# First projections from raw fp32 chunks, the gates' arithmetic on GpSimd, and other ranks in the mixer of a two-layer decoder trunk

## The chip, the core and the metric

The kernel runs on one core of a Trainium2 chip. The metric is the time of one execution in device microseconds; the time before is 652.5 us, the median of three runs (650.82, 652.57, 652.5). PE is TensorE, DVE is VectorE, ACT is ScalarE, POOL is GpSimd; SP is the engine whose queue issues most of the loads.

## What is computed

Two layers on x of 256 tokens by 1024, all in float32. Layer 0 mixes tokens with a gated DeltaNet, layer 1 with softmax attention; after each mixer and after each SwiGLU (hidden width 2816) stands a residual with alpha = sqrt(2) and a LayerNorm. The change touches layer 0's mixer:

```python
proj = x @ w_in                       # q, k, v, z: 1024 columns each; b and a: 8 each
qkv = silu(causal_depthwise_conv(qkv, w_conv))      # width 4
q = l2_normalize(q) * 128 ** -0.5;  k = l2_normalize(k)
beta = sigmoid(b_logit)
g = -(exp(a_log) * softplus(a_in + dt_bias))        # the gates
gc = cumsum(g) in chunks; decay[c, s] = exp(gc[c] - gc[s]) for s <= c
low = strict_tril((k * beta) @ k.T * decay)         # triangular solve per chunk
sol = triangular_solve(low, [v * beta, k * beta * exp(gc)])
o = (chunked recurrence with sol, q, k, decay)
o = o * rsqrt(mean(o * o) + 1e-6) * norm_g * silu(z)
x = LN(alpha * x + o @ w_out)
```

## The kernel before

**Weights.** All weights lie in DRAM as 204 units of 128 x 1024 floats in the order of use, two units to a chunk of 1 MB. A chunk is loaded into one of three `raw` buffers (`Stream.load`; the first two chunks in pieces by `Stream.first`). Each unit is then split for full precision: ACT rounds it to `hi` (`Stream.head`), DVE makes `lo = raw - hi` (`Stream.rest`), into one of nine buffer pairs; the first `NSMALL` units are split in two halves. x is split alike, into `xTh` and `xTl`. A product of 128 x 128 weights with 256 tokens is three fp32r matmuls: hi by xTh, hi by xTl, lo by xTh; a unit of eight is 24 (`proj_w`).

**Layer 0's mixer.** `ORDER` is the order of the projections: `k0` is two units (256 columns of k), `z0` four units in two passes. After each part a job runs beside the stream: `keys`, `queries`, `values` do the convolution (`conv_silu`: two ACT copies with scale, six DVE scalar_tensor_tensor from PSUM, then a Silu that waits for the mark `decay`), transposes (`ptk`, `ptq`, `ptv`) and small products. `gram` is a product of kT with itself, times `dT` it gives `gdT`; `blocks` inverts its 16 x 16 diagonal blocks on DVE with trips through DRAM (`dG`, `dX`, `dXT`; `cB` is its first DVE step); `doubling` grows the inverse with small products (`py`, `pz0`, `pz1`); `core` is the recurrence; then `wo` follows.

**The gates.** `pgate` is x times the 16 gate columns in fp32; a DVE copy, two products (`pgate2`) and a copy give `ba`; `gates` then works out g on tiles of 128 x 16: exponentials on ACT, the rest on DVE, a series for the softplus, down to `gg`. Four products (`pcum`) sum it up. Their first row goes to DRAM (`d1`, the DMA `d<-gT`), comes back spread over all partitions (`grow`, four loads, one in each job `decay`), is masked by four POOL selects into `dT` and passes through 16 ACT exponentials. When all are done, `grow` itself is exponentiated and `decay` is marked.

**Order.** There is no scheduler on the chip that could reorder: each engine runs its instructions in the order in which the program writes them, and waits on semaphores. That order is worked out when the program is written: `Clock` keeps a modelled time for each engine from the costs in `act`, `tt`, `ptt`, `select`, `mm`, and `dma`; after each matmul of the main stream `tick` looks which jobs' next steps would be ready and takes, on each engine, the one with the lowest rank. Ranks are `PR` (by kind of job), `GET_PRIO` (for splits, by how far ahead of their use they are) and `LOAD_PRIO` (chunk loads on SP). PSUM is two groups of four banks, `A` and `P`.

**The start.** Eight warm-up products; on SP's queue `wg` (the gate weights) and the first pieces of the chunks; on ACT's queue four loads of x and two of `al` (a_log and dt_bias), then the activation table's load. The first two units and x are split in halves as they come, with five warm-up products after each of the first two pairs of gate products.

Of the kernel before, what the change touches and what calls it, by code (L numbers as in the profile page):

```python
# [12 lines left out]
F32 = mybir.dt.float32  # L13
# [5 lines left out]
P = 128  # L19
# [4 lines left out]
H = 8  # L24
# [12 lines left out]
NWARM = (8, 5, 5, 0, 0)  # L37
NSMALL = 40
# [87 lines left out]
def trunk_kernel(ctx: ExitStack, tc: tile.TileContext, xT, xtok, wst, wgate, conv, alog, dtb,  # L126
# [28 lines left out]
    def act(out_, in_, func=AF.Copy, after=0.0, **kw):  # L155
        base = 0.09 + 0.00083 * width(out_)
        base += 0.06 * any(not isinstance(kw.get(a, 1.0), float) for a in ("scale", "bias"))
        base += 0.095 * ("accum_out" in kw)
# [35 lines left out]

    def pmemset(out_, v):
# [34 lines left out]
    class Stream:  # L230
        def __init__(self):
            self.raw, self.hi, self.lo = {}, {}, {}
            self.loaded = self.piece = self.freed = 0
            self.late, self.first_at = [], {}
# [7 lines left out]
            self.pieces[1:3] = self.pieces[2:0:-1]  # L242
# [44 lines left out]
        def head(self):  # L287
            u, a, b = self.pieces[self.piece]
            if a == 0:
                self.hi[u] = wp.tile([P, UCOLS], F32R, tag="hi", name=f"hi{u}", bufs=NHL)  # L290
                self.lo[u] = wp.tile([P, UCOLS], F32R, tag="lo", name=f"lo{u}", bufs=NHL)
# [78 lines left out]
    def tick():  # L370
        polled = set()
        while True:
# [4 lines left out]
            for eng in ("pe", "act", "dve", "pool", "sp"):  # L377
# [10 lines left out]
                elif eng == "sp" and ws.pend:  # L388
# [240 lines left out]
    warm(NWARM[0])  # L629
# [3 lines left out]
    xt = []  # L633
# [6 lines left out]
    al = cst.tile([P, 2, H], F32, name="al")  # L640
    nc.scalar.dma_start(al[:, 0], bass.AP(tensor=alog.tensor, offset=alog.offset, ap=[[0, P], [1, H]]))
    nc.scalar.dma_start(al[:, 1], bass.AP(tensor=dtb.tensor, offset=dtb.offset, ap=[[0, P], [1, H]]))
    ws.first(4, 11.5)
    ws.first(5, 13.0)
# [7 lines left out]

    ea = cst.tile([P, H], F32, name="ea")
    act(ea[:, 0:1], ones[:, 0:1], AF.Exp)
    T.update(act=4.5, pe=0.0)
# [16 lines left out]
    T["pool"] = 3.0  # L672
# [20 lines left out]
    def gates(pg):  # L693
# [14 lines left out]
        tt(xa, ba[:, 1], al[:, 1, :, None].to_broadcast([P, H, 2]), OP.add)  # L708
# [4 lines left out]
        act(ea, al[:, 0], AF.Exp)  # L713
        yield

        ts(s2, at, 2.0, None, OP.add)
        ts(gt[:, 0], gt[:, 0], 1.0, None, OP.add)
        recip(s2, s2)
        recip(beta, gt[:, 0])
        tt(at, at, s2, OP.mult)  # L720
        ts(xa, xa, 0.0, None, OP.max)
        tt(s2, at, at, OP.mult)
        tt(xa, xa, ea[:, :, None].to_broadcast([P, H, 2]), OP.mult)
        ts(acc, s2, 1.0 / 15, None, OP.mult)
        tt(at, at, ea[:, :, None].to_broadcast([P, H, 2]), OP.mult)
# [19 lines left out]
        dma(nc.sync, d1, gT)  # L745
        bT = cst.tile([16, P], F32, name="bT")
# [10 lines left out]
        yield from wait(*[("decay", j) for j in range(4)])  # L757
        g1 = grow.rearrange("p (h c) t -> p h c t", c=2)[:, :, 1]
        act(g1, g1, AF.Exp)
        mark("decay")  # L760
# [13 lines left out]
        select(cmask[:, P:], cmask[:, P:], [[-1, P]], OP.is_ge, NEG, 1)  # L774

    def decay(j, d1, ngc):
# [4 lines left out]
            bass.AP(tensor=d1.tensor, offset=d1.offset + 512 * j, ap=[[0, P], [1, 512]]), 0.73)  # L781
# [34 lines left out]

    kT = b8("kT", [P, H, SEQ])
# [240 lines left out]
    def values(j, ps, pname):  # L1058
        vt = yield from t2(f"vt{j}", (P, 2, SEQ))
        yield from conv_silu(vt, ps, pname, 16 + 2 * j, f"v{j}")  # L1060
        yield from wait("nk", "q")
# [14 lines left out]
    def core(G):  # L1076
# [4 lines left out]
        zz = big_t["zz"]  # L1081
# [8 lines left out]
        def fin(c, pname, ps):  # L1090
# [9 lines left out]
            yield from wait(("z", G, c))  # L1100
            for i in range(4):
# [42 lines left out]
    def gates_z(G, t, pz):  # L1144
# [364 lines left out]
```

## Time and profile before

| | us |
|---|---|
| median of three timed runs | 652.5 |
| the profiled execution | 651.09 |
| its span, from the first to the last instruction | 649.3 |
| PE busy in the span | 636.8 |
| DVE, ACT, POOL busy | 458.4, 366.7, 29.9 |

The span is what the profile's rows cover; the rest of the profiled execution's time lies around it. A matmul's end in the rows is modelled, so groups that overlap in the rows can be read by the distance of their starts.

### The profile page before, as it was taken

What the parts mean: (1) busy time and instruction counts of PE and PEld (TensorE: products, weight loads), DVE (VectorE), ACT (ScalarE), POOL (GpSimd) and SP (SyncE); (2) the same over time, 40 slices, a digit from 0 to 9 for tenths busy, and PEclk for the clock granted to TensorE, in tenths of its full rate; (3) what the DMA queues carried; (4) which work ended last, traced back from release to release, by engine and by line L of the source; (5) the groups of instructions that cost most, each with busy time, mean ns of one, the idle gap of its engine ahead of it and who ended that gap; (6) DMA issues with size and microseconds to landing.
All of it is one profiled execution on the core that took longest, in us unless ns stands there. A gap on an engine that the chain in (4) does not pass through costs nothing.

```text
span 649.3 us, 9918 instructions
## 1 busy us (share of the span) xinstructions
PE 636.8 (98%) x3791; PEld 555.1 (85%) x3791; DVE 458.4 (71%) x802; ACT 366.7 (56%) x719; POOL 29.9 (5%) x43
## 2 busy tenths in 40 slices
PE   8999999999999999999999999999999999999995
PEld 7999898898888888888888888888888888888884
DVE  3878999368976666666649679887886666666645
ACT  4689757874465555555535468765475555555510
POOL 1043100021000000000000000000000000000001
PEclk9999999899999999999999999999999999999998
DMA  8576478145655555555545474352565555555302
GB/s 285 194 257 165 138 211 249 50 155 179 251 219 216 175 188 186 192 195 187 198 191 194 143 268 174 132 194 70 191 258 200 191 194 195 195 194 189 136 0 66
DMA packets 37024, 117.91 MB, mean 182 GB/s; under 512 B 20464, under 2 KB 21648, under 8 KB 23536
## 3 DMA queue, kind: packets, MB, share of 16 engines
q1 hardware_dynamic: 35376, 115.54, 50.6%
q10 hardware_dynamic: 1440, 1.58, 0.8%
q8 instruction: 30, 0.49, 0.3%
q0 software_dynamic: 160, 0.15, 0.2%
q14 instruction: 18, 0.15, 0.1%
HBM read 115.41 MB, written 1.85 MB: 181 GB/s over the span
## 4 chain that ended last, share of the span: by engine, by line
PE 91%; issue 6%; ACT 1%; DVE 1%; POOL 0%; DVEq 0%; POOLq 0%; ACTq 0%
PE pf L213 31%; PE acc L213 17%; PE pqk L213 7%; PE pz L213 4%; PE pu L213 4%; PE pcvalues L213 4%; PE bo L213 3%; PE wo L213 3%; PE pg L213 3%; PE pv L213 3%; PE pcqueries L213 2%; PE pl L213 2%; PE po L213 2%; PE sc L213 1%; PE lnT L216 1%
## 5 line engine op out<-in xcount | busy, mean ns | idle before, releaser
L172 DVE TENSOR_TENSOR lo<-raw,hi 128x1024 fp32r<-128x1024 f32 (+1 forms) x244 | 252.8, 1047 | 116.4 <-ACT hi L166 114.7
L166 ACT ACTIVATE hi<-raw 128x1024 fp32r<-128x1024 f32 (+1 forms) x244 | 219.7, 924 | 165.4 <-issue 59.2
L213 PE MATMUL pf<-xT,hi 128*128 128x512 f32 x576 | 143.8, 391 | 0.0
L213 PEld LDWEIGHTS pf<-xT,hi 128*128 128x128 f32 x576 | 104.6, 189 | 19.4
L213 PE MATMUL acc<-hi,ht 128*128 128x512 f32 x320 | 99.0, 391 | 0.0
L213 PEld LDWEIGHTS pf<-xT,lo 128*128 128x128 f32 x576 | 78.6, 190 | 5.6
L213 PE MATMUL pf<-xT,lo 128*128 128x256 f32 x576 | 80.8, 283 | 0.0
L213 PEld LDWEIGHTS acc<-hi,ht 128*128 128x128 f32 x320 | 59.0, 188 | 11.4
L213 PE MATMUL acc<-lo,ht 128*128 128x512 f32 x160 | 62.3, 390 | 0.0
L213 PEld LDWEIGHTS acc<-lo,ht 128*128 128x128 f32 x160 | 30.0, 188 | 6.3
L213 PE MATMUL pqk<-xT,hi 128*128 128x512 f32 x128 | 34.7, 401 | 0.0
L172 DVE TENSOR_TENSOR sgw<-sgw,pf 128x256 f32<-128x256 f32 x72 | 29.8, 415 | 1.6 <-ACT sgw L166 1.6
L193 POOL TENSOR_TENSOR lnst<-lnst,nhalf 128x1 f32<-128x1 f32 x8 | 8.5, 1057 | 488.4 <-DVE lnst L180 488.4
L166 ACT ACTIVATE sgw<-pf 128x256 f32<-128x256 f32 x72 | 26.4, 366 | 0.0
L213 PEld LDWEIGHTS pqk<-xT,hi 128*128 128x128 f32 x128 | 22.8, 189 | 3.7
L213 PE MATMUL pckeys<-xT,hi 128*128 128x256 f32 x128 | 23.7, 286 | 0.5 <-ACT hi L166 0.5
L213 PE MATMUL pcqueries<-xT,hi 128*128 128x256 f32 x128 | 23.8, 287 | 0.0
L213 PE MATMUL pcvalues<-xT,hi 128*128 128x256 f32 x128 | 23.1, 283 | 0.0
L176 DVE SCALAR_TENSOR_TENSOR y<-y,lnst,gb 128x512 f32<-128x512 f32 (+1 forms) x36 | 22.7, 685 | 0.0
L213 PE MATMUL pz<-hi,xT 128*128 128x512 f32 x64 | 22.1, 417 | 0.0
L213 PEld LDWEIGHTS pckeys<-xT,hi 128*128 128x128 f32 x128 | 19.9, 191 | 1.1 <-ACT hi L166 1.1
L213 PE MATMUL pu<-hi,xT 128*128 128x512 f32 x64 | 20.4, 395 | 0.0
(233 smaller groups left out, 999.5 us busy)
## 6 DMA issues: line engine op xcount, KB each, us to landing
raw<-wst SPq DMA_DIRECT2D x100, 1024.0 KB, 4.8
gb<-lnp SPq DMA_DIRECT2D x4, 1024.0 KB, 7.0
xraw<-xT ACTq DMA_DIRECT2D x4, 256.0 KB, 5.9
raw<-wst SPq DMA_DIRECT2D x4, 256.0 KB, 5.4
raw<-wst SPq DMA_DIRECT2D x2, 512.0 KB, 6.4
grow<-d SPq DMA_DIRECT2D x4, 256.0 KB, 6.3
y<-xtok SPq DMA_DIRECT2D x1, 1024.0 KB, 7.1
out_dram<-y ACTq DMA_DIRECT2D x4, 128.0 KB, 1.9
```

Of the source, the lines that this page charges most:

```text
L166: return op("act", cost, lambda: nc.scalar.activation(out_, in_, func, **kw), after)
L172: return dve(out_, 0.06 + 0.00105 * rate * width(out_), lambda: nc.vector.tensor_tensor(out_, a, b, op=alu), after)
L176: lambda: nc.vector.scalar_tensor_tensor(out_, a, s, b, op0=op0, op1=op1), **kw)
L193: op("pool", cost, lambda: nc.gpsimd.tensor_tensor(out_, a, b, op=alu))
L213: op("pe", cost, lambda: nc.tensor.matmul(out_, lhs, rhs, start=start, stop=stop, **kw))
L216: op("pe", 0.11, lambda: nc.tensor.transpose(out_, src, ident[:src.shape[0], :src.shape[0]]))
```

## The change

The first halves of units 0 and 1 are multiplied in fp32 straight from the loaded chunk and from raw x (`first_step`); the second halves and x are split in a new order, and the warm-up products after the first eight are gone. All eight gate products stand together, before the last step of units 0 and 1. `al` is loaded on POOL's queue, `wg` after the first chunk, and the table load stands between the second and third load of x. The gates' elementwise work goes to POOL except the two reciprocals. No chunk load may be written on SP between the write of `d1` and the last load of `grow` (`held`). `gates` waits for the four `decay` jobs only after its own DMAs. Costs in the model, ranks and `ORDER` are new (`v0` after `q0`, `v1` and `z0` after `q3`), and 56 units are split in halves in place of 40.

```diff
-NWARM = (8, 5, 5, 0, 0)
-NSMALL = 40
+NWARM = 8
+NSMALL = 56
-GET_PRIO = (3.5, 3.3), (4.5, 0), (12.5, 5.9), (17.0, 3.6), (18.0, 11.7)
-LOAD_PRIO = 6.35
+GET_PRIO = (-3.5, 3), (2.5, 4.3), (17.5, 8.6), (19.0, 3.6), (33.5, 8.9)
+LOAD_PRIO = 9.85
-PR = dict(gates=2.5, decay=5.2, blocks=0, doubling=1, core=2.5, out0=3.2, z=1, k=2.6, q=4.0, v=1.4, late=3.0, ln=0, ffn=5.6, att=4.4)
+PR = dict(gates=0, decay=6.4, blocks=0, doubling=6.0, core=0, out0=0, z=2.8, k=1.1, q=5.7, v=2.3, late=5.0, ln=0, ffn=5.6, att=4.4)
-ORDER = "k0 k1 k2 k3 q0 q1 q2 q3 z0 v0 v1 v2 v3 z1"
+ORDER = "k0 k1 k2 k3 q0 v0 q1 q2 q3 v1 z0 v2 v3 z1"
...
+    def pts(out_, a, s0, s1, op0, op1=None):
+        kw = {} if op1 is None else dict(op1=op1)
+        op("pool", 0.15 + 0.0025 * width(out_), lambda: nc.gpsimd.tensor_scalar(out_, a, s0, s1, op0=op0, **kw))
...
-        op("pool", 0.12 + 0.0015 * width(out_),
+        op("pool", 0.12 + 0.00205 * width(out_),
...
-                elif eng == "sp" and ws.pend:
+                elif eng == "sp" and ws.pend and not ws.held:
...
-    nc.sync.dma_start(wg, wgate)
-    for n in range(4):
+    for n, t in enumerate((4.2, 4.7, 6.0, 7.0)):
         k = slice(2 * n, 2 * n + 2)
         nc.scalar.dma_start(xraw[:, k], xT[:, k])
-        xt += [4.7 + 1.45 * n] * 2
-        ws.first((0, 2, 1, 3)[n], 5.4 + 1.5 * n)
-    nc.scalar.dma_start(al[:, 0], bass.AP(tensor=alog.tensor, offset=alog.offset, ap=[[0, P], [1, H]]))
+        ws.first((0, 2, 1, 3)[n], t)
+        if n == 1:
+            act(ea[:, 0:1], ones[:, 0:1], AF.Exp)
+    nc.sync.dma_start(wg, wgate)
+    nc.gpsimd.dma_start(al[:, 0], bass.AP(tensor=alog.tensor, offset=alog.offset, ap=[[0, P], [1, H]]))
...
-        tt(xa, ba[:, 1], al[:, 1, :, None].to_broadcast([P, H, 2]), OP.add)
+        ptt(xa, ba[:, 1], al[:, 1, :, None].to_broadcast([P, H, 2]), OP.add)
...
-        ts(acc, s2, 1.0 / 15, None, OP.mult)
-        for m in (13, 11, 9, 7, 5, 3):
-            stt(acc, acc, 1.0 / m, s2, OP.add, OP.mult)
-        stt(acc, acc, 1.0, at, OP.add, OP.mult)
-        stt(gg, acc, -2.0, xa, OP.mult, OP.subtract)
+        pts(acc, s2, 1.0 / 15, 1.0 / 13, OP.mult, OP.add)
+        for m in (11, 9, 7, 5, 3, 1):
+            ptt(acc, acc, s2, OP.mult)
+            pts(acc, acc, 1.0 / m, None, OP.add)
+        ptt(acc, acc, at, OP.mult)
+        ptt(gg, acc, nea[:, :, None].to_broadcast([P, H, 2]), OP.mult)
...
         dma(nc.sync, d1, gT)
+        then(lambda: setattr(ws, "held", 4))
...
+    def first_step(u, n):
+        raw = ws.raw[0][:, u * UCOLS:(u + 1) * UCOLS].rearrange("p (k c) -> p k c", c=P)
+        for k in (2 * n, 2 * n + 1) if n < 2 else ():
+            mm(first_ps[:, u], raw[:, k], xraw[:, k], start=u == k == 0, stop=False, skip_group_check=True)
+        if n < 2:
+            return
+        hi, lo = (c[u].rearrange("p (k c) -> p k c", c=P) for c in (ws.hi, ws.lo))
+        for i, (a, b) in enumerate(((hi, xTh), (hi, xTl), (lo, xTh))):
+            for k in (2 * n, 2 * n + 1):
+                mm(first_ps[:, u], a[:, k], b[:, k], start=False, stop=k == KT - 1 and i == 2, skip_group_check=True)
...
+    x_part(0)
+    x_part(1)
+    w_part(0)
+    x_part(2)
+    w_part(1)
+    x_part(3)
```

What stands in a row on PE at the program's start, first before, then after (`pckeys` is the bank of units 0 and 1):

```order
L627 MATMUL pwarm<-ones 128x128 x8
L213 MATMUL pgate<-xraw,wg 32x256 x2
L627 MATMUL pwarm<-ones 128x128 x5
L213 MATMUL pgate<-xraw,wg 32x256 x2
L627 MATMUL pwarm<-ones 128x128 x5
L213 MATMUL pckeys_154<-xT_136,hi_164 128x256 x2
L213 MATMUL pckeys_154<-xT_136,lo_165 128x256
```

```order
L635 MATMUL pwarm<-ones 128x128 x8
L221 MATMUL pckeys_154<-xraw,raw_90 128x256 x8
L221 MATMUL pckeys_154<-xT_136,hi_159 128x256 x4
L221 MATMUL pckeys_154<-xT_136,lo_160 128x256 x2
L221 MATMUL pckeys_154<-xT_136,hi_165 128x256 x4
L221 MATMUL pckeys_154<-xT_136,lo_166 128x256 x2
L221 MATMUL pgate<-xraw,wg 32x256 x8
L221 MATMUL pckeys_154<-xT_136,hi_159 128x256 x4
L221 MATMUL pgate_205<-sum_115,l_148 128x16 x2
```

Eight products from `raw` come first, all gate products stand behind them, and `pgate2` follows after four more. `pcum` stood after 15 products of unit 4 and now stands between units 3 and 4.

On DVE behind the second reciprocal of the gates, before and after (`lo` is a split of weights, `cyk` the convolution of k, `gt` the gates' tile, `gT` the copy that waits for `pcum`):

```order
L186 RECIPROCAL beta<-gt 128x16
L172 TENSOR_TENSOR gt<-gt 128x16
L180 TENSOR_SCALAR gt<-gt 128x16
L176 SCALAR_TENSOR_TENSOR cyk_251<-pckeys_154,cw,cyk_251 128x254
L172 TENSOR_TENSOR gt<-gt 128x16
L172 TENSOR_TENSOR gt<-gt,ea 128x16
L176 SCALAR_TENSOR_TENSOR cyk_251<-pckeys_154,cw,cyk_251 128x253
L180 TENSOR_SCALAR gt<-gt 128x16
L172 TENSOR_TENSOR lo_292<-raw_105,hi_291 128x512
```

```order
L186 RECIPROCAL beta<-gt 128x16
L176 SCALAR_TENSOR_TENSOR cyk_237<-pckeys_154,cw,cyk_237 128x255
L172 TENSOR_TENSOR lo_257<-raw_107,hi_256 128x512
L176 SCALAR_TENSOR_TENSOR cyk_237<-pckeys_154,cw,cyk_237 128x255
L172 TENSOR_TENSOR lo_257<-raw_107,hi_256 128x512
L176 SCALAR_TENSOR_TENSOR cyk_237<-pckeys_154,cw,cyk_237 128x254 x2
L172 TENSOR_TENSOR lo_272<-raw_107,hi_271 128x512
L176 SCALAR_TENSOR_TENSOR cyk_237<-pckeys_154,cw,cyk_237 128x253
L172 TENSOR_TENSOR lo_272<-raw_107,hi_271 128x512
L176 SCALAR_TENSOR_TENSOR cyk_237<-pckeys_154,cw,cyk_237 128x253
L172 TENSOR_TENSOR lo_315<-raw_206,hi_314 128x512
L183 COPY gT<-pcum 16x128
```

The gates' small operations are gone from DVE; five splits stand between the reciprocals and `gT`.

On POOL from the masks of `dT` on, before and after (`d` is the write of the beta rows, `bB` their way back, `dX` and `dXT` are cleared in DRAM):

```order
L200 AFFINE_SELECT dT<-grow 128x512 x4
L224 DMA d_384<-bT 16x128
L224 DMA bB<-d_384 64x16 x2
L196 MEMSET l_148 64x256
L224 DMA dX<-l_148 64x16x16
```

```order
L193 TENSOR_TENSOR gg<-gt,nea 128x16
L232 DMA d_346<-bT 16x128
L208 AFFINE_SELECT dT<-grow 128x512 x3
L232 DMA bB<-d_346 64x16 x2
L204 MEMSET l_148 64x256
L232 DMA dX<-l_148 64x16x16
L232 DMA dXT<-l_148 64x16x16
L204 MEMSET misc 128x256
L204 MEMSET misc 128x16
L204 MEMSET cmask 128x256
L208 AFFINE_SELECT cmask<-cmask 128x128
L208 AFFINE_SELECT dT<-grow 128x512
```

Ahead of `gg` stand 23 more operations of the gates; the fourth select has moved behind the gates' DMAs and memsets. On SP, `d1` stood two chunk loads ahead of the four loads of `grow`, and now stands right ahead of them.

## Rows read from the trace of the kernel before

**Rows 1.** The page's first part: busy time of each engine.
```profile
PE 636.8 (98%) x3791; PEld 555.1 (85%) x3791; DVE 458.4 (71%) x802; ACT 366.7 (56%) x719; POOL 29.9 (5%) x43
```
**Rows 2.** Stretches: length, busy PE, PEld, DVE, ACT, POOL; granted clock, DMA share, GB/s.
```profile
113.80:117.00 3.20, 3.20 (x13) 2.69 (x12) 2.29 (x7) 2.99 (x6) 0.00 (x0) 0.50 0.57 236
...
160.00:200.00 40.00, 40.00 (x201) 33.59 (x200) 33.71 (x41) 22.66 (x28) 0.99 (x1) 1.00 0.63 230
```
**Rows 3.** Who PE waited for: us in total, times, longest.
```profile
PE gram L213 <- ACT kT L166: 1.2, 1, 1.2
...
PE py L213 <- issue: 0.7, 1, 0.7
PE pcum L213 <- DVE gg L176: 0.7, 1, 0.7
```
**Rows 4.** The first 24 us in order of time: start, us, engine, instruction, idle before.
```profile
6.87 1.28 ACT L166 ACT_TABLE_LOAD   x1 [6.87 <-DMA xraw<-xT]
...
7.60 1.38 PE L627 MATMUL pwarm<-ones 128*128 128x128 f32 x10
...
8.27 0.61 ACT L166 ACTIVATE xT<-xraw 128x512 fp32r<-128x512 f32 x1
...
9.46 0.59 PE L213 MATMUL pckeys<-xT,hi 128*128 128x256 f32 x2 [0.48 <-ACT hi L166]
...
13.09 0.64 PE L213 MATMUL pgate<-xraw,wg 128*32 128x256 f32 x8
...
23.02 0.84 ACT L166 ACTIVATE cyk<-pckeys,cw 128x256 f32<-128x256 f32 x2 [1.48 <-PE pckeys L213]
```
**Rows 5.** The loads of x, and stretches of the first 8 us (GB/s last).
```profile
L637 ACTq DMA_DIRECT2D xraw<-xT x4: 414/452/453, 0.8 to 2.2; - x4
...
DMA to landing us min/median/max: 4.3/5.9/7.0
...
0.00:4.00 4.00, 2.96 (x14) 2.96 (x15) 0.00 (x0) 0.00 (x0) 1.89 (x14) 1.00 0.46 110
4.00:6.00 2.00, 1.47 (x10) 0.87 (x10) 0.00 (x0) 0.00 (x0) 0.00 (x0) 1.00 0.99 360
6.00:8.00 2.00, 2.00 (x17) 1.47 (x17) 0.00 (x0) 1.13 (x1) 0.00 (x0) 1.00 1.06 399
```
**Rows 6.** The chain that ended last: fp32 products of 128 columns, fp32r ones of 256.
```profile
73.14 0.89 PE pa L213 x8
...
82.77 23.03 PE pcvalues L213 x192
```
**Rows 7.** DVE in order of time: the end of the gates' chain.
```profile
25.11 0.18 DVE L176 SCALAR_TENSOR_TENSOR gg<-gt 128x16 f32<-128x16 f32 x1
```
**Rows 8.** POOL and DVE in order of time; groups of `pow`, ns min/median/max.
```profile
1.49 1.01 POOL L663 TENSOR_SCALAR_AFFINE_SELECT sum<-sum 128x16 f32<-128x16 f32 x4
...
L193 POOL TENSOR_TENSOR lnst<-lnst,nhalf x8: 907/952/1433, 158.3 to 643.2; 128x1 f32<-128x1 f32 x8
...
L193 POOL TENSOR_TENSOR ms<-ms,nhalf x4: 1008/1014/1391, 134.5 to 146.3; 128x4 f32<-128x4 f32 x4
...
37.53 1.30 POOL L200 TENSOR_SCALAR_AFFINE_SELECT dT<-grow 128x512 f32<-128x512 f32 x1 [34.69 <-DMA grow<-d]
37.66 0.67 DVE L172 TENSOR_TENSOR lo<-raw,hi 128x512 fp32r<-128x512 f32 x1
...
39.83 0.63 POOL L200 TENSOR_SCALAR_AFFINE_SELECT dT<-grow 128x512 f32<-128x512 f32 x1
```
**Rows 9.** SP, POOL and ACT in order of time, on the way to the mark `decay`.
```profile
27.90 3.48 SPq L250 DMA_DIRECT2D raw<-wst  x2
...
46.02 1.05 POOL L224 DMA_DIRECT2D bB<-d  x2 [3.87 <-DMA d<-bT]
...
50.20 0.29 POOL L200 TENSOR_SCALAR_AFFINE_SELECT cmask<-cmask 128x128 f32<-128x128 f32 x1
...
47.17 0.63 ACT L166 ACTIVATE kT<-cyk 128x512 f32<-128x512 f32 x1
```

More of the change, by code (lines that the diff above doesn't have):

```diff
@@ L157, in act @@
         base += 0.06 * any(not isinstance(kw.get(a, 1.0), float) for a in ("scale", "bias"))
-        base += 0.095 * ("accum_out" in kw)
+        base += 0.095 * ("accum_out" in kw) + 0.035 * (not isinstance(kw.get("bias", 1.0), float))
         def cost():
@@ L233, in __init__ @@
             self.loaded = self.piece = self.freed = 0
-            self.late, self.first_at = [], {}
+            self.late, self.first_at, self.held = [], {}, 0
             self.arrive, self.ready, self.job = {}, {}, Job()
@@ L288, in head @@
             u, a, b = self.pieces[self.piece]
-            if a == 0:
+            if u not in self.hi:
                 self.hi[u] = wp.tile([P, UCOLS], F32R, tag="hi", name=f"hi{u}", bufs=NHL)
@@ L651, in trunk_kernel @@
     nc.sync.dma_start(rp, rope)
-    ea = cst.tile([P, H], F32, name="ea")
-    act(ea[:, 0:1], ones[:, 0:1], AF.Exp)
-    T.update(act=4.5, pe=0.0)
+    T.update(act=4.1, pe=0.0)
     ident = cst.tile([P, P], F32, name="ident")
@@ L756, in gates @@
         mark("e2")
[L757 to L760, printed above, removed]
         yield
@@ L774, in gates @@
         select(cmask[:, P:], cmask[:, P:], [[-1, P]], OP.is_ge, NEG, 1)
+        yield from wait(*[("decay", j) for j in range(4)])
+        g1 = grow.rearrange("p (h c) t -> p h c t", c=2)[:, :, 1]
+        act(g1, g1, AF.Exp)
+        mark("decay")
+        yield
     def decay(j, d1, ngc):
@@ L780, in decay @@
         dma(nc.sync, grow[:, c].rearrange("p a b -> p (a b)"),
-            bass.AP(tensor=d1.tensor, offset=d1.offset + 512 * j, ap=[[0, P], [1, 512]]), 0.73)
+            bass.AP(tensor=d1.tensor, offset=d1.offset + 512 * j, ap=[[0, P], [1, 512]]), 0.95)
+        then(lambda: setattr(ws, "held", ws.held - 1))
         yield
@@ L1060, in values @@
         yield from conv_silu(vt, ps, pname, 16 + 2 * j, f"v{j}")
-        yield from wait("nk", "q")
+        yield from wait("nk", *["q"] * z_first)
         pt = yield from to_tokens(vt, f"ptv{j}")
@@ L1144, in gates_z @@
     def gates_z(G, t, pz):
+        yield from wait("decay", *["q"] * (not z_first))
         if "zz" not in big_t:
             big_t["zz"] = b8("zz", [P, 2, D])
-        yield from wait("decay")
         act(big_t["zz"][:, t, 512 * G:512 * G + 512], pz, AF.Silu)
@@ L1179, in trunk_kernel @@
     first_ps = main_bank("P", "pckeys0").rearrange("p (a b) -> p a b", a=2)
[L1180 to L1201 removed]
+    def first_step(u, n):
[8 more added lines that the diff above has]
+                mm(first_ps[:, u], a[:, k], b[:, k], start=False, stop=k == KT - 1 and i == 2, skip_group_check=True)
+                if n == 3:
+                    tick()
@@ new lines, in trunk_kernel, with made, x_part, w_part @@
+    at = {}
+    def made(name):
+        at[name] = T["dve"] + LAT - 0.48
+    def x_part(n):
+        c = slice(2 * n, 2 * n + 2)
+        split(xTh[:, c], xTl[:, c], xraw[:, c], xt[2 * n])
+        made(("x", n))
+    def w_part(u):
+        ws.head()
+        ws.rest()
+        made(("w", u))
+    x_part(0)
[4 more added lines that the diff above has]
+    x_part(3)
+    for n in range(4):
+        for u in range(2):
+            if n == 3 and u == 0:
+                for k in range(KT):
+                    c = 32 * (k % 4)
+                    mm(pg[c:c + 32, :SEQ], wg[:, k], xraw[:, k], start=(k < 4), stop=(k >= 4))
+                spawn(gates(pg), PR["gates"])
+            ck.main.t0 = max(xt[2 * n], ws.first_at[2 * u]) if n < 2 else max(at["x", n], at["w", u])
+            first_step(u, n)
@@ L1205, in trunk_kernel @@
     ui[0] = 2
-    spawn(gates(pg), PR["gates"])
     for part in ORDER.split():
```

61 lines of the change are left out of this document (26 added, 35 removed).

## The prediction

> **What bounds the kernel now.** I read the head of the page first, then the busy time by stretches, then who TensorE waited for, and last the first 50 us in order of time. TensorE (PE) is busy for 98% of the span [rows 1]: every other engine matters only where PE waits for it. From 160 us on there is not one idle microsecond on PE in a stretch of 40 [rows 2], and the instructions there are the same before and after (only the halving of units 40 to 55 and the ranks differ). So the change can pay, or cost, only before the mixer's end, in four places: the start; two waits of the stream of projections (`pcum` 0.7 us, `gram` 1.2 us); one wait of 0.7 us at `py` [rows 3]; and a stretch after `py` in which the granted clock is at the lower of its two levels, 0.50 from 113.8 to 117.0 [rows 2]. PE is in order, so a wait moves all that stands behind it, and a lead won at the start lasts only as far as the next instruction that waits for something which did not get earlier. That question decides this case.
>
> **The start.** Before, PE's first projection runs at 9.46, though the first part of x has been in since about 5.1 (issued at 0.8, landed 4.3 later) [rows 4, 5]. What is late is ScalarE: its table load waits until 6.87, since the issues of x and of the two 4 KB `al` loads stand ahead of it on its queue, and its first split follows at 8.27 [rows 4]. After: `al` goes to GpSimd's queue, the table load stands between the second and third load of x, and PE's first eight products take the raw chunk and raw x in fp32, with no split ahead of them.
>
> When is the data there? Bytes moved by 4, 6 and 8 us are 0.44, 1.16 and 1.96 MB [rows 5]. I let the two queues share equally; before, the first x part would then be complete at the 0.52 MB mark (4.2 us), and it was seen 0.9 later. After, the first four pieces of 0.26 MB are x0, chunk 0 of unit 0, x1, chunk 0 of unit 1: pairs complete at 4.2, 5.7, 7.0 and a little after 8, so in hand at 5.1, 6.6, 7.9 and 9.3 with that lag, and 0.9 earlier without it. An fp32 product (two instructions in the rows) of 128 columns costs 0.22 us (four in 0.89), so one of 256 about 0.44; an fp32r one 0.12 (192 in 23.03) [rows 6]. Eight fp32 products are 3.6 us in place of 24 fp32r ones at 2.9: 0.7 us more work, paid in time in which PE only warmed up before.
>
> Step by step with the lag: first product 5.1, second unit's at 6.6, four steps of 0.89 done at 9.3; twelve fp32r products behind the splits of the third parts to 11.1; the eight gate products at twice 0.64 us for four [rows 4] end at 12.4. Without the lag 11.0 (the splits then press). I take **P = 11.7** for the end of the gate products; before it was 13.09 + 0.64 = 13.7. Behind them stand a copy that `pgate2` waits for (some 0.9 us with `pgate2`) and twelve products, so unit 2 starts at 14.05, and units 2 and 3 (48 x 0.12 = 5.8) end at 19.8. Before, unit 3 ended at 23.0, when ScalarE took it up [rows 4]. **Lead 3.1 us, bounds 2.4 to 3.9.**
>
> **The gates on GpSimd.** This is where the lead meets its first wait. `pcum` now stands right behind unit 3, 1.8 us of products earlier in the stream than before, and waits for `gg`, the end of the gates' chain. Before, `gg` was done at 25.3, 11.6 us after the gate products [rows 7]. After: copies, `pgate2` and ScalarE's four small functions take the chain to P + 3.1, three GpSimd operations and two reciprocals to P + 4.6; then 20 GpSimd operations that each need the one before. No such operation is in the trace. The nearest row is a chain of four small selects, each waiting for the last: 0.25 us each [rows 8]. The other end is a `pow` on the same engine, 0.91 us for one element [rows 8]. I take 0.25, because width and waiting are alike: 5 us, `gg` at P + 9.6. To that comes DVE: a select beside a DVE subtraction with two inputs in SBUF took 1.30 us, one beside operations on PSUM 0.63, and the difference is that subtraction's 0.67 [rows 8]. Five such subtractions stand on DVE between the reciprocals and the copy that waits for `pcum`, so 0 to 3.3 us. I take 0.7: **`gg` at P + 10.3 = 22.0, and PE waits 2.3 us** at 19.8, against 0.7 before. Net loss 1.6; bounds -0.7 (no wait) to +4.2 (3.3 us of blocking).
>
> The Trainium skill, page SBUF — State Buffer, section Who interferes with whom, speaks against this placement: a VectorE instruction with two SBUF inputs and a GpSimd instruction that reads SBUF exclude each other for the whole instruction. The rows agree for the first select (1.30 = 0.63 + 0.67). By that rule taken fully, all five subtractions block, PE waits 4.9 us and the sum below rises by 2.6 us. The page GPSIMD Engine Reference, section Engine selection, has two-input elementwise work on GpSimd about twice as slow as on VectorE; from the 0.18 us of `gg` on DVE that is an estimate of 0.36 an operation, and the sum would rise by 2.5 us. No run here shows it for such an operation.
>
> DVE is rid of some 20 small operations, but stands still while it waits for GpSimd and for `pcum`; I cost that at nothing, since the splits of units 4 and 5 stand ahead of the waiting copy. If they came late, units 4 and 5 would wait by as much.
>
> **The decay chain and `gram`.** SP's queue before: two raw loads of 1 MB stood between the write of the decay rows and their four broadcast loads, 3.5 us [rows 9]. After, `held` keeps raw loads out of that gap. What is new on GpSimd: the gates' DMAs and memsets now stand ahead of the fourth `dT` select; from 46.0 to 50.5 before [rows 9], they cost the chain 4.5 us. From `gg` at 22.0: rows written at about 25, broadcasts in at 28 to 31, fourth select done at about 38, four exponentials, `grow`, the table and the first Silu at about 42, against 47.8 before [rows 9]. PE comes to `gram` after 13.1 units, one and a half units further on than before: 22.1 + 0.8 for `pcum`'s products + 9.1 x 2.88 = 49. The 1.2 us wait goes, with 6 us to spare. **Gain 1.2, bounds 0 to 1.2.** What is late next is the blocks' chain through DVE and DRAM, which gates `py`. It starts no earlier, since `gram` stands further on; but the order puts DVE's part of it ahead of more of the splits, and `py` stands 1.6 us later in PE's work (twelve more transposes, five fewer `pz` products). ScalarE's copies of the transposed values now stand shortly ahead of `py`. **Gain 0.4, bounds -0.5 to 0.7.**
>
> **The end of the mixer.** The small products stand closer together after: 16 of `py`, then 48 of `pz0`/`pz1`, where a large product of `pz` lay between before. The clock was at 0.50 for 3.2 us [rows 2], worth 1.6 us at half speed. It may stay, go, or come a second time: **0, bounds -1.6 to +1.6**. Halved splits of 16 more units cost DVE and ScalarE some tenths each; they run beside a PE that has no gap there [rows 2], nothing. New ranks elsewhere: nothing, and their price if wrong is a new PE wait in the feed-forward stages.
>
> **Sum.** -3.1 + 1.6 - 1.2 - 0.4 + 0 = -3.1 us. The profiled execution took 651.1 us (649.3 of it the span), so 648.0. The three timed runs lie -0.3 to +1.5 us about it, 0.9 on average (their median 1.4 above); with that average I forecast **648.9 us**.
>
> **Rivals.** (a) The lead is eaten at `pcum`: DVE's subtractions block all they can, or an operation costs 0.36. Then 648.9 + 2.5 = 651.4, no difference that can be told. For: [rows 8], and each of 23 operations adds up. Against: the third select, 0.63, shows GpSimd running freely beside operations on PSUM, and half of DVE's work there is of that kind. (b) Slower: a GpSimd arithmetic operation has the price of `pow`, 0.91, which is the same instruction [rows 8]. Then 23 x 0.66 = 15 us more, `gg` at 37, and about 664. It decides from some 0.4 us an operation on, where PE waits 3.1 us longer than in the sum and all four terms are used up. Against: one and four elements of `pow` cost alike, so that price looks like the function's, and the selects cost a quarter. (c) The clock: without the warm-up products that ran until 9.0 [rows 4], fp32 products run at the lower level for a while, or the bursts at `py` lower it twice. Up to 3.6 + 1.6 us: 652 to 654. Against: from 5.1 on PE stands for 0.6 us at most, less than before. (d) The change doesn't bring its start: pieces land no earlier and PE gains 1 us of the 3.1; about 651.
>
> **How the numbers follow.** Forecast 0.60, (a) 0.22, (d) 0.06, (c) 0.06, (b) 0.06. A measurement of this kernel can tell about 0.3%, 2 us, so faster means under 650.5. The forecast's own spread (start 0.8 either way, `pcum` 2, clock 1.6) makes 645 to 652, of which a tenth lies above the bound; a quarter of (a) and half of (d) lie below it: faster 0.62, same 0.29, slower 0.09 (all of (b), half of (c)). The range takes in (a), (d) and part of (c): 644.8 to 653.
>
> **What would show it.** PE's first `pckeys` near 5.1 and unit 3 done near 19.8; a wait of PE at `pcum` for GpSimd, 1 to 4 us, with single GpSimd operations near 0.25 us, longer where a `lo` runs; no wait at `gram`. Wrong if GpSimd operations are near 0.9, if the granted clock falls before 15 us, or if a new PE wait stands behind 150 us.

## Result and the profile after

The changed kernel takes 659.1 us (median of 14 runs, 658.0 to 659.6), the kernel before 653.7 on the same chips: **1.0063 times as long by the means (659.1 and 654.9), 95% interval 1.0037 to 1.0089. It is slower, by 0.6%; forecast were 648.9 us and a range up to 653.0.** The executions of the kernel before differ among themselves by the time that TensorE spends at its lower clock (experiment 1), so medians stand below beside executions of like clock. The profiled execution took 659.6 us, its span 657.9, 8.6 more than before.

From 160 us on little changed: `wo` starts 8.6 us later than before, and PE's last instruction 9.0. So the loss lies ahead of that, and I went first to what PE waited for (the columns of [rows 3]):

```profile
PE pcum L221 <- POOL gg L193: 4.0, 1, 4.0
PE pcvalues L221 <- DVE cyq L176: 1.4, 1, 1.4
...
PE ptv L224 <- ACT vt L166: 0.8, 1, 0.8
```

The wait at `gram` is gone, the one at `py` too, as forecast (1.2 and 0.7). `pcum` went from 0.7 to 4.0, and two waits are new. The start in order of time (the columns of [rows 4]) shows why `pcum` is that late:

```profile
1.73 1.28 ACT L166 ACT_TABLE_LOAD   x1 [1.73 <-PEq L1541]
...
5.39 5.99 PE L221 MATMUL pckeys<-xraw,raw 128*128 128x256 f32 x16 [0.55 <-DMA xraw<-xT]
...
10.43 0.63 ACT L166 ACTIVATE hi<-raw 128x512 fp32r<-128x512 f32 x1 [2.42 <-DMA raw<-wst]
...
13.81 1.07 PE L221 MATMUL pgate<-xraw,wg 128*32 128x256 f32 x16
```

The table load is early and PE's first product is at 5.39, just as the steps said (5.1). But the second half of unit 0 is split only at 10.43, after 2.42 us of waiting for its load, and the gate products end at 14.9 instead of 11.7. The 256 KB pieces of the chunk took 7.3 us (median) from issue to landing, before 5.4. The lead at the end of unit 3 is nil: ScalarE takes it up at 23.04, before at 23.02 [rows 4].

The gates' chain on GpSimd, a part of it in order of time:

```profile
19.61 0.52 POOL L197 TENSOR_SCALAR gt<-gt 128x16 f32<-128x16 f32 x1
20.21 0.22 POOL L193 TENSOR_TENSOR gt<-gt 128x16 f32<-128x16 f32 x1
20.52 0.65 POOL L197 TENSOR_SCALAR gt<-gt 128x16 f32<-128x16 f32 x1
21.25 0.22 POOL L193 TENSOR_TENSOR gt<-gt 128x16 f32<-128x16 f32 x1
...
26.61 0.22 POOL L193 TENSOR_TENSOR gg<-gt,nea 128x16 f32<-128x16 f32 x1
```

An operation takes 0.22 to 0.26 us, and 0.52 to 0.65 where a `lo` runs on VectorE (from 19.37, 20.38, 21.76, 22.75 and 23.74 on): five such in this chain, 1.8 us more in all. With some 0.07 us between operations the 20 take 7.8 us.

The last view is the granted clock by stretches (columns as in [rows 2]):

```profile
25.00:30.00 5.00, 3.12 (x15) 2.71 (x16) 1.31 (x4) 1.67 (x3) 1.50 (x7) 0.69 0.48 198
30.00:35.00 5.00, 5.00 (x42) 5.00 (x42) 4.97 (x12) 0.00 (x0) 1.17 (x2) 0.96 0.71 189
...
120.00:125.00 5.00, 4.94 (x95) 4.11 (x91) 3.36 (x6) 4.89 (x11) 0.00 (x0) 0.75 0.38 157
125.00:130.00 5.00, 5.00 (x43) 4.23 (x42) 0.06 (x1) 1.68 (x7) 0.00 (x0) 0.50 0.64 213
130.00:135.00 5.00, 5.00 (x28) 4.61 (x27) 4.24 (x10) 2.05 (x5) 0.00 (x0) 0.50 0.00 0
135.00:140.00 5.00, 5.00 (x39) 4.83 (x38) 0.71 (x4) 3.16 (x14) 0.00 (x0) 0.88 0.00 0
```

PE is at 1.2 GHz (0.50) for 3.4 us behind the wait at `pcum`, and for 13.6 us from 122.5 on; before it was one spell of 3.4 us [rows 2] (the last microseconds of either span, in which PE has nothing to do, are left out). At half speed that is up to 1.7 and 6.8 us, before 1.7. Before the clock fell at 122.5, PE had run this (order of time; short groups in which products of two kinds alternate are left out):

```profile
118.48 1.00 PE L221 MATMUL py<-misc,gdT 32*32 32x32 f32 x29
...
119.82 0.98 PE L221 MATMUL pz<-wa,y 32*32 32x32 f32 x29
120.79 0.59 PE L221 MATMUL pz<-y,wa 32*32 32x32 f32 x13
...
121.31 0.98 PE L221 MATMUL pz<-wa,y 32*32 32x32 f32 x29
122.22 0.99 PE L221 MATMUL pz<-hi,xT 128*128 128x512 f32 x2
123.27 1.97 PE L221 MATMUL py<-X,gdT 64*64 64x64 f32 x16
```

3.7 us of products on 32 rows and 32 columns of the array without one large product between. Before, a large product stood between any two such bursts; a part of it:

```profile
119.64 0.98 PE L213 MATMUL pz<-wa,y 32*32 32x32 f32 x29
...
120.74 0.48 PE L213 MATMUL pz<-hi,xT 128*128 128x512 f32 x1
121.15 0.59 PE L213 MATMUL pz<-y,wa 32*32 32x32 f32 x13
```

The account of the 8.6 us: waits before 160 us 8.3 in place of 4.9 (+3.4), clock up to +6.8. That is 1.6 us too much. Not every instruction takes twice as long at the lower level (16 of `py` on 64 rows 1.97 us, at the upper 1.14), so the clock's part, as what is left, is nearer to 5.

### The profile page after: what moved, and what is told of

It is laid out like the page before. It is cut to its first block, busy times and chain, and to the rows that moved or that the text cites. A ratio compares the mean times of both kernels' runs of the same rounds, so it can differ in the third digit from the quotient of the medians.

```text
span 657.9 us, 9885 instructions
## 1 busy us (share of the span) xinstructions
PE 642.1 (98%) x3763; PEld 559.2 (85%) x3763; DVE 456.5 (69%) x799; ACT 367.3 (56%) x733; POOL 36.9 (6%) x69
## 4 chain that ended last, share of the span: by engine, by line
PE 88%; DVE 6%; ACT 2%; issue 1%; DMA 1%; POOL 1%; SPq 0%; DVEq 0%; ACTq 0%
PE pf L221 31%; PE acc L221 17%; PE pqk L221 7%; PE pu L221 4%; PE pcqueries L221 3%; PE bo L221 3%; PE pv L221 3%; PE pcvalues L221 3%; PE pg L221 2%; PE pckeys L221 2%; PE pl L221 2%; PE po L221 2%; DVE lo L172 2%; PE pz L221 2%; PE wo L221 1%
## 5 line engine op out<-in xcount | busy, mean ns | idle before, releaser
L166 ACT ACTIVATE sgw<-pf 128x256 f32<-128x256 f32 x72 | 26.3, 366 | 0.2 <-PE pf L221 0.2
L221 PE MATMUL pcvalues<-xT,hi 128*128 128x256 f32 x128 | 23.9, 286 | 1.4 <-DVE cyq L176 1.4
L221 PE MATMUL pckeys<-xT,hi 128*128 128x256 f32 x112 | 21.3, 294 | 0.6 <-DVE xT L172 0.3
L221 PEld LDWEIGHTS pcvalues<-xT,hi 128*128 128x128 f32 x128 | 19.9, 191 | 1.6 <-ACT cyv L166 1.5
```

The costliest lines, as they stand in the source:

```text
L166: return op("act", cost, lambda: nc.scalar.activation(out_, in_, func, **kw), after)
L221: op("pe", cost, lambda: nc.tensor.matmul(out_, lhs, rhs, start=start, stop=stop, **kw))
```

## Experiments

Where I moved an operation to another engine, the costs by which the order is planned were left as they were, so TensorE's instructions stand in the order of the kernel that was edited; where that order differs, it is said.

**1. The kernel before, again.** 

> The kernel before, unchanged, run again to see what its own executions do. Its executions so far lie in two groups, near 651.5 and near 658.5 us. Theory: the upper group has the same loss as the changed kernel, a long spell of the lower clock at the end of the mixer; then its executions near 658 show a mean granted clock near 0.985, those near 651 one near 0.995, and one us of time goes with 0.0015 of clock. Rival: the groups have nothing to do with the clock; then the mean clock is alike in both.

Theory held. Of this run's 12 executions six have a mean clock of 0.983 (657.7 to 659.3 us), two 0.991, four 0.995 or more (650.2 to 651.6). Of 35 executions of the kernel before that ran beside the first experiments, 11 have a mean clock of 0.993 to 0.996 and 651.2 us on average, 12 have 0.991 or 0.992 (652.6), 7 have 0.988 (655.1), 5 have 0.983 (658.4). The profile of one that took 658.1:

```profile
120.00:130.00 10.00, 10.00 (x110) 8.42 (x108) 2.72 (x6) 5.54 (x18) 0.00 (x0) 0.61 0.01 2
130.00:140.00 10.00, 10.00 (x54) 9.47 (x54) 0.42 (x1) 3.43 (x9) 0.00 (x0) 0.53 0.00 0
```

It is the long spell of the changed kernel, at the same place, and the waits are those of [rows 3] but for one of 0.5 us. So the low clock at the mixer's end was in the kernel before all along, in some executions. The changed kernel has it in all 14 (0.984 to 0.987). Against executions of before that have it as well, the change costs 0.7 us (in the profiles both are at the lower level for 17.1 us, PE's idle end left out: 17.1 in one spell before, 3.4 and 13.6 after); against those without, 8.

**2. The gate operations on VectorE.**

```diff
-        ptt(at, at, s2, OP.mult)          # and 23 more: nc.gpsimd
+        vtt(at, at, s2, OP.mult)          # same place, nc.vector
```

> The changed kernel with the 23 small gate operations issued to VectorE instead of GpSimd, at the same places of the order, so that TensorE's order is the same to the last instruction. Theory (each GpSimd operation costs 0.25 us and as much again beside a two-input VectorE subtraction): 23 operations at about 0.18 us take 4 us instead of 10, gg comes near 22, TensorE's wait at pcum falls from 4.0 to 0 to 1 us and the half clock behind it (27 to 30 us) goes; about 655 us. Rival (the chain's length is set by what stands ahead of it, not by the operations): the wait at pcum stays above 3 us and the time at 659. If the wait goes but the lead is lost at the next wait, the time stays at 658 to 659 though pcum is clean.

658.9 us, and PE still waits:

```profile
PE pcum L228 <- DVE gg L204: 3.7, 1, 3.7
```

My theory fell. VectorE needs 0.17 us for one operation, but in its in-order queue splits and convolution steps stand between them:

```profile
20.46 0.18 DVE L204 TENSOR_TENSOR gt<-gt 128x16 f32<-128x16 f32 x1
20.55 0.48 DVE L176 SCALAR_TENSOR_TENSOR cyk<-pckeys,cw,cyk 128x255 f32<-128x255 f32 x1
20.95 0.17 DVE L208 TENSOR_SCALAR gt<-gt 128x16 f32<-128x16 f32 x1
21.15 0.18 DVE L204 TENSOR_TENSOR gt<-gt 128x16 f32<-128x16 f32 x1
21.24 0.69 DVE L172 TENSOR_TENSOR lo<-raw,hi 128x512 fp32r<-128x512 f32 x1
21.84 0.17 DVE L208 TENSOR_SCALAR gt<-gt 128x16 f32<-128x16 f32 x1
```

`gg` ends at 26.3 here, at 26.8 on GpSimd. Changing the engine alone gains 0.5 us of the chain; the 20 operations, some 0.2 us apart where nothing stands between them, would take 4 us and took 6.5.

**3. The chain packed.** So the next kernel lets nothing in between: 13 operations on VectorE, in the fused form of the kernel before, back to back.

```diff
-        ptt(at, at, s2, OP.mult)
-        ... 19 more
+        def chain():
+            v = nc.vector
+            v.tensor_tensor(at, at, s2, op=OP.mult)
+            ...
+            for m in (13, 11, 9, 7, 5, 3):
+                v.scalar_tensor_tensor(acc, acc, 1.0 / m, s2, op0=OP.add, op1=OP.mult)
+            ...
+        op("pool", 20 * (0.15 + 0.0025 * width(gg)), chain)
```

> The changed kernel with the 20 chained gate operations replaced by 13 on VectorE (its fused form, as before the change), issued one right behind the other with no subtraction between them; every other instruction stands where it stood. Theory (what makes TensorE wait at pcum is that each small operation lets other work in between, on GpSimd by the blocking and on VectorE by the queue; packed, 13 x 0.2 = 2.6 us are enough): gg near 22 instead of 26.8, no wait at pcum, no low clock at 27 to 30 us; the subtractions of units 4 and 5 come 2.6 us later and cost at most 1 us; the lead of 4 is kept to the end unless another wait takes it, 655. Rival (what follows takes it back: the conv steps that PE waits for at 105 and the chain to the doubling do not come earlier): pcum clean, but time 658 to 659.

653.6 us (652.6 to 655.9), 5.5 less than the changed kernel; ratio to before 0.9967 (0.9936 to 0.9998). `gg` ends at 22.0, PE does not wait at `pcum`, and from 20 to 30 us it is busy throughout at full clock:

```profile
20.00:30.00 10.00, 10.00 (x85) 9.66 (x84) 9.69 (x29) 5.64 (x12) 0.00 (x0) 1.00 0.54 191
```

The waits at `pcvalues` (1.4) and `ptv` (0.8) and the low spell (here 116.8 to 130.5 us) are as in the changed kernel. This execution has another low spell at 7.6 to 11.0 us, while PE waits for loads and splits; its gate products end at 14.4 all the same. The wait of 4.0 and up to 1.7 for the clock behind it were to be had, and 5.5 came. Two things were changed at once: nothing stands between, and seven operations are fewer. At 0.2 us each the seven are 1.4 of the 4.3 us by which `gg` is earlier than in experiment 2; the rest is mostly what stood between. Executions of the kernel before, beside it, that have the long spell too take 658.0, 4.4 more than this.

**4. The bursts apart.**

```diff
     def doubling(G):
+        if G:
+            yield from wait(("lv32", 0))
```

From the first `pz` on the order differs: large products stand between all the bursts of tiny ones. 

> The changed kernel with the second half of the doubling held back until the first has its 32-row level, so that 512-column products stand between the four bursts of 32x32 products and nothing else changes before them. Theory (a long unbroken burst of tiny products, 3.7 us here, is what sends the clock to its lower level, and 14 us at that level cost 6.8 us): the low spell at 122 to 136 us shrinks to 4 us or less, as it was before, and the time falls by about 5 us to 654. Rival (the clock falls for another reason, such as the spell of waits and transfers around it): the low spell stays about 14 us and the time within 1 us of 659, or grows by the longer chain of the second half.

654.1 to 655.4 us in five executions (clock 0.989 to 0.994), 658.9 to 662.0 in five (0.983 to 0.986). In the profiled one, of 655.4 us, the spell is gone:

```profile
120.00:130.00 10.00, 9.95 (x191) 8.36 (x190) 6.08 (x11) 9.03 (x23) 0.00 (x0) 1.00 0.43 158
130.00:140.00 10.00, 10.00 (x90) 9.64 (x88) 4.49 (x15) 6.52 (x26) 1.03 (x2) 1.00 0.62 224
```

Spreading the bursts pays 4 to 5 us where it works, in half of the executions.

**5. Large products put in between.** Ten 512-column products whose results are overwritten, in the changed kernel and in the kernel before.

```diff
+        fill(2, pz)      # nc.tensor.matmul(pz, xT2[:, 0, 0, :P], xT2[:, 0], ...) twice
```

> The changed kernel with ten extra products of 512 columns, whose results are overwritten, at the head of the eight bursts of tiny products (two ahead of each pz burst, one ahead of each other). They cost TensorE 10 x 0.22 = 2.2 us and change nothing of the computation. Theory (tiny products without large ones between them bring the lower clock): the low spell of 14 us gets shorter or goes, 659 - 6.8 + 2.2 = 654.5 if it goes in every execution, and a mean clock of 0.992 or more. Rival (it is the waits and the chain around the bursts): spell as before and 661.

> The kernel before with the same ten extra products. Its executions lay in groups at clocks of 0.995, 0.991, 0.988 and 0.983 (651, 652.6, 655 and 658.5 us). Theory (tiny bursts lower the clock, and it hangs on the execution how long): nearly all executions come into the highest clock, at 651 + 2.2 = 653, and the group near 658 vanishes. Rival: the groups stay, each 2.2 us later, with a third or more of the executions below 0.99.

In the kernel before it did for the most part what the theory said: 653.0 to 656.3 us, eight executions of twelve at 0.996 to 0.998, four at 0.991, none near 0.983. Ten products cost about what they bring: 0.9997 times before (0.9966 to 1.0028). In the changed kernel it did not: two of six at 0.994 (657.5, 657.8), four at 0.979 to 0.981 (664.2 to 666.8). There the bursts of `py1`, `pz0` and `pz1` stand right behind one another but for the two added products ahead of each `pz`, and in this order these were too few. Neither edit alone settles it; experiment 8 joins them.

**6. The start.** One more warm-up product closes PE's gap ahead of the first fp32 product.

```diff
-NWARM = 8
+NWARM = 9
```

> The changed kernel with nine warm-up products instead of eight, which closes the 0.55 us in which TensorE stood still before its first fp32 product. Theory (landing): the fp32 products may run at 0.21 us an instruction instead of 0.43 and be over by 9 us, but the halves of the chunk that the splits need land at 10.4 as before, so the gate products end at 14.9 all the same and the time stays at 659. Rival (the clock alone holds the start back): the gate products end near 13 and the time falls by 2 us. Third: the fill changes nothing, the products run at 0.43 us until 9.5 again.

659.2 us. The 16 fp32 instructions took 4.9 us in place of 6.0 and were over at 10.1, and the gate products still ended at 14.4, within the 14.4 to 14.9 of the five other profiles with `al` on GpSimd's queue: the splits wait for the loads. Then the loads:

```diff
-    nc.gpsimd.dma_start(al[:, 0], ...)
-    nc.gpsimd.dma_start(al[:, 1], ...)
+    nc.sync.dma_start(al[:, 0], ...)
+    nc.sync.dma_start(al[:, 1], ...)
```

> The changed kernel with the two small broadcast loads of al issued on SyncE's queue, behind units 2 and 3, instead of on GpSimd's. Theory (packets of GpSimd's queue, 24 to 37% of the transfer engines' time between 6 and 8 us for almost no bytes, slow the pieces of x and of the chunk): the second half of unit 0 lands before 9.5 instead of 10.4, the gate products end near 14 instead of 14.9, gg and unit 4 come 1 us earlier, and TensorE still waits 4 us at pcum because that wait moves along with the start; time 658. Rival (the slow stretch comes from the order of the pieces and from the fourth load of x, issued only at 5.0): first split of the chunk at 10.4 again, no change.

658.3 us (657.6 to 658.8), 0.8 less. The half of unit 0 is split 1.7 us earlier than in the profile of the changed kernel and the gate products end at 13.2 in place of 14.9, while PE waits 4.1 us at `pcum`, which moved along. Over all profiles the gate products end at 14.6 on average with `al` on GpSimd's queue (six) and at 13.3 with `al` on SP's (four), so 1.4 us is the better figure:

```profile
8.75 0.63 ACT L166 ACTIVATE hi<-raw 128x512 fp32r<-128x512 f32 x1 [0.38 <-DMA raw<-wst]
...
12.14 1.07 PE L221 MATMUL pgate<-xraw,wg 128*32 128x256 f32 x16
```

What the two 4 KB loads cost on GpSimd's queue stands in the transfer view of the changed kernel, from 7 to 8 us (packets, MB, share of 16 engines): 23 packets, no bytes to speak of, 37% of the time.

```profile
q0 software_dynamic: 23, 0.00, 37.1%
q1 hardware_dynamic: 63, 0.12, 30.8%
q10 hardware_dynamic: 58, 0.11, 28.6%
```

> As the last one, and the four loads of x all issued ahead of ScalarE's table load. Theory (the fourth load of x, issued at 5.0 behind the table load, is the last thing the splits wait for): it is issued by 2.7 us, the split of the fourth part starts near 10.5 instead of 12.0, and the gate products end 1 to 1.5 us earlier than with the al loads moved alone; time about 657. Rival (bytes, not issues, set the landing; a fifth load waits in the queue whoever is first): the gate products end within 0.3 us of the kernel with the al loads moved alone.

658.2 us, the split of the half unit at 8.83, the gate copy at 13.37 against 13.28: the rival. The issue of the fourth load of x was not what held the start.

**7. Does a lead at the start last?** The same edit in the kernel before, where the two loads held up ScalarE's table load.

> The kernel before with one edit: its two al loads moved from ScalarE's queue to SyncE's, behind units 2 and 3, so that the table load no longer waits for them at 6.87. Nothing else moves. It asks whether a lead at the start lasts. Theory: table load near 2.7, first split of x at 5.2 to 6, gate products end 2 us earlier than 13.7, gg and pcum with them, and the lead of about 2 us is there at 160 us still: best executions 649, median 2 us below that of before. Rival (the lead is lost at the wait for gram or py, whose chains do not start earlier): gate products earlier, but best executions still at 651.

Median 651.9 (before, beside it: 653.6; ratio 0.9979, 0.9937 to 1.0021, so not told apart by medians). Table load at 2.67, first split at 5.11, `gg` at 23.9 in place of 25.3. The four best executions, at a clock of 0.993 to 0.997, took 649.6 to 650.7, where before, beside it, needs 651.0 to 652.3 at 0.993 to 0.996: on average 650.1 and 651.5, so 1.4 us lasted. The waits at `pcum`, `gram` and `py` are those of [rows 3], neither shorter nor longer: here a lead moved the whole chain along.

**8. The mended kernel.** The changed kernel with `al` on SP's queue, the packed chain and the bursts apart, without and with four large products ahead of the `pz` bursts.

> The changed kernel with three edits together: the al loads on SyncE's queue, the 13 packed gate operations on VectorE, the second doubling held back. Theory: start -1.5, pcum -4 and its low clock -1.6, the low spell at the end gone in more than half of the executions: best executions 649 to 651, others 655. Rival: what is won ahead of the mixer's end is lost there; best executions at 654 as with the bursts apart alone.

Six of twelve executions at 0.995 to 0.998 and 649.2 to 650.6 us, six at 0.981 to 0.989 and 654.6 to 658.6; 0.9972 times before (0.9931 to 1.0012). The start and `pcum` pay (1.8 us of waiting left there), a wait of 0.9 us at `gram` is back, and the clock is again a matter of the execution.

> The mended kernel with four extra 512-column products, two ahead of each pz burst (0.9 us), whose results are overwritten. Theory (it is the share of tiny products in the few us around the bursts that decides): 12 of 12 executions come near a clock of 0.995, at 650 to 651.5, and none stays near 0.983. Rival (in the new order the low level is set off by the waits of TensorE at 90 to 105 us and by the chain, not by the bursts): about half of the executions stay at 654 to 659, as in the mended kernel.

**650.2 us, ten of twelve executions between 649.9 and 651.3 at 0.994 to 0.998 (the others 653.1 at 0.992 and 654.7 at 0.988); 0.9951 times before (0.9920 to 0.9983).** The profile keeps the waits at `pcum` (1.6), `pcvalues` and `ptv`, and has no low spell:

```profile
120.00:130.00 10.00, 10.00 (x130) 9.05 (x127) 5.38 (x12) 6.54 (x16) 0.00 (x0) 1.00 0.35 129
130.00:140.00 10.00, 10.00 (x83) 9.65 (x82) 4.56 (x18) 6.28 (x26) 2.03 (x2) 1.00 0.75 294
```

The waits at `pcvalues` and `ptv` are still there and the spell is not; the two kernels differ by four products alone. So it is the bursts, not the waits ahead of them, that the low clock at the mixer's end hangs on. Whether the size of the added products does it or only the distance that they put between the bursts, no run separates.

**9. The kernel before, mended likewise.** `al` on SP's queue and the four large products; then its gate chain packed as well.

> The last one with four extra 512-column products, two ahead of each pz burst (0.9 us), whose results are overwritten. Theory: as in the kernel before with ten of them, the group at a clock of 0.983 vanishes; best executions 0.9 us above those without them, median 1 us or more below. Rival: four are too few, and the groups stay.

**650.5 us, all twelve executions between 650.0 and 651.6 (0.994 to 0.998); 0.9934 times before (0.9904 to 0.9964).** With the mended kernel of experiment 8 it is the fastest here, and it has nothing of the change in it; `al` is moved, but to another queue than there.

> The kernel before with al on SyncE's queue and the four extra products, and with its 14 chained gate operations on VectorE issued one right behind the other. Theory (a chain that lets nothing in between ends earlier, and each of the three waits of TensorE behind it, pcum 0.7, gram 1.2 and py 0.7, stands at the end of that chain): gg at 22 instead of 24.5, the wait at pcum goes, gram's gets shorter, and the median falls by 1 to 2 us below the 650.5 of the kernel without packing. Rival (gram waits for work behind pcum on GpSimd and ScalarE that is not earlier): only pcum's 0.7 goes, or nothing, 649.8 to 650.5.

651.8 us, 0.9971 times before (0.9936 to 1.0005): no gain over the kernel without packing. `gg` ends 3 us earlier and the wait of 0.7 at `pcum` is gone, but PE waits 1.4 for a split that the packed chain pushed back, and the waits at `gram` and `py` are where they were:

```profile
PE pckeys L213 <- DVE lo L172: 1.4, 1, 1.4
PE gram L213 <- ACT kT L166: 1.2, 1, 1.2
...
PE py L213 <- issue: 0.7, 1, 0.7
```

Packing pays where the chain is last (4.0 us in the changed kernel), not where something else is.

## Why the prediction was wrong

- **The start, -3.1: failed, at the landing of the pieces.** The order of steps was right (table load, first product, the fp32 products in the cover of the loads). The pairs were to be in hand at 5.1, 6.6, 7.9 and 9.3; that came from the bytes moved per us before, shared equally. After, 2.1 MB were moved in the first 10 us in place of 2.6 (122 and 301 GB/s in the two stretches of 5 us, 158 and 362 before). I had priced the moved `al` loads on ScalarE's side, where they went away, and at nothing on the queue they went to: 1.4 us there (experiment 6). For the rest, some 1.6 us at the gate products (13.3 against 11.7), no run names a cause; the second pair was in hand at 7.3, and with `al` on SP's queue at 7.5, where the steps said 6.6. For the start rival (d) was the case, at a chance of 0.06.
- **`pcum`, +1.6: mechanism right, sizes off.** PE waits there for GpSimd, as forecast. The chain took 12.0 us from the gate products instead of 10.3: 0.07 us between operations, which the price of 0.25 left out, and 1.8 of blocking where I took 0.7. The Trainium skill (SBUF — State Buffer, section Who interferes with whom) describes that exclusion, and the rows bear it out: 0.52 to 0.65 beside a subtraction of two SBUF inputs, 0.22 to 0.26 elsewhere. It explains 1.8 us of the chain and not the wait; on VectorE it was as long (3.7). The wait grew by 3.3 us because `pcum` stands 1.8 us earlier among PE's products and `gg` came 1.5 us later than before (26.8 against 25.3), at the end of a chain that mixes with other work on either engine. The lead that did not come has no part in it: with 1.7 us of it the wait was 4.1.
- **Behind `pcum`: left out.** Behind the wait of 4.0 us PE was at the lower level for 3.4 us, up to 1.7 us more; packed, both go (experiment 3). All seven profiles with 3.7 to 4.4 us of waiting at `pcum` have such a spell right behind it, those with 0 to 1.8 us have none. The prediction thought of the clock at the start and at `py` only.
- **`gram`, -1.2, and `py`, -0.4: both waits went, at `gram` with some luck.** Two things were to help there: PE comes later, by one and a half units, and its input is ready earlier, at 42 against PE's 49. Only the first held. The input was ready at 54.8 and PE came at 55.6, late itself by the lost lead, the wait at `pcum` and the low clock, so 0.8 us were to spare and not 6:

```profile
54.15 0.63 ACT L166 ACTIVATE kT<-cyk 128x512 f32<-128x512 f32 x1
...
55.56 1.06 PE L221 MATMUL gram<-kT 128*128 128x128 f32 x8
```

  From `gg` on the chain took 28.0 us where the steps said 20: the fourth select, behind the gates' DMAs and memsets, ended at 45.2 (forecast about 38), and splits on ScalarE stood in what followed. In the packed kernel 0.4 us were to spare, and in the mended one 0.9 us of the wait was back.
- **New ranks elsewhere, 0: failed.** 2.2 us of new waits. `v0` and `v1` now stand among the queries, and their convolution steps queue on VectorE behind the blocks' products and behind splits: the step that frees a bank for `pcvalues` ran at 104.10, after three splits from 102.30 on, and PE stood until 104.72:

```profile
102.30 1.89 DVE L172 TENSOR_TENSOR lo<-raw,hi 128x512 fp32r<-128x512 f32 x3
104.10 0.47 DVE L176 SCALAR_TENSOR_TENSOR cyq<-pcqueries,cw,cyq 128x253 f32<-128x253 f32 x1
```

  The prediction had looked for such waits only in the feed-forward stages. All ten profiles with the new order have these two waits (1.4 and 0.8), none with the order of before has the one at `pcvalues`; why they arise is read from the trace, and no run undid the order alone.
- **The clock at the end, 0, bounds -1.6 to +1.6: failed.** The text had the right place and the right reason ("the bursts at `py` lower it twice"), and as a bound the 3.2 us of one profile. The spell was 13.6 us, up to 5.1 us more lost. The kernel before has spells as long in some executions; neither its one trace nor the three timed runs known then (650.8 to 652.6) showed that.

Against the forecast that is 3.1 at the start, 1.7 at `pcum`, up to 1.7 behind it, 2.2 for the ranks, up to 5.1 at the end, less 0.3 at `py`: at most 13.5, where 11.6 were measured; the difference is the clock's bound, as above. The rivals had been priced one at a time; here (d) at the start, most of (a) at `pcum` and the clock's share of (c) at the bursts came together. What stays open is how dense the bursts must be: spread alone they left the long spell in half of the executions, filled alone (in the changed order) in four of six, both together in none of twelve below 0.988.

## What to carry to other kernels

Price a moved instruction on the queue that receives it, and a chain of small operations by what its engine lets in between, before asking which engine is faster. Look at the granted clock stretch by stretch, and at the time of every execution against its mean clock: a spell that one profile showed at 3 us was 17 in another execution of the same kernel. A large product or two between bursts of tiny ones, even a useless one, can be the cheapest instruction of a kernel: here four of them (0.9 us) and two moved loads gave 0.66%.

## What the hardware showed unexpectedly

- The low spells differ from profile to profile: behind `pcum` 3.4 us in the changed kernel and 6.8 with the bursts apart, at the mixer's end 3.4 and 17.1 us (122 to 139) in two executions of the kernel before, 13.6 in the changed kernel, 10.2 with one more warm-up product. Executions of one kernel fall into distinct clocks (0.995, 0.991, 0.988, 0.983), not into a continuum.
- At the start the granted clock reads 1.00 in the changed kernel while products run at half the later pace: the first 11 fp32 instructions followed one another at 0.40 to 0.59 us, the last five at 0.21 to 0.22. Which ones do differs from execution to execution: the kernel with the bursts apart has the same start and ran them faster, and the packed one, whose clock does read 0.50 from 7.6 to 11.0, ran those in that stretch at 0.42 to 0.45. The groups by line of the changed kernel (busy us, mean ns of one, idle time before):

```profile
L221 PE MATMUL pckeys<-xraw,raw 128*128 128x256 f32 x16 | 6.0, 552 | 0.5 <-DMA xraw<-xT 0.5
```

  and of the kernel with the bursts apart:

```profile
L221 PE MATMUL pckeys<-xraw,raw 128*128 128x256 f32 x16 | 4.0, 392 | 1.4 <-DMA raw<-wst 0.7 <-DMA xraw<-xT 0.7
```

  Both end their gate products at 14.9, since the splits wait for loads.
- Two loads of 4 KB on GpSimd's queue took 24, 37 and 12% of the transfer engines' time in three successive us (6 to 9); with them on SP's queue the half of unit 0 was split at 8.7 to 9.0 us (four profiles) in place of 9.8 to 10.5 (six).
